# WKV recurrence on one core: another order of the drain, and two pieces of VectorE's work in other places

## The chip, the cores and the metric

The kernel runs on one core of a Trainium2 chip. The metric is the device time of one execution in microseconds (us). The core has a matrix engine (TensorE, "PE" in the profile, with its weight loads as "PEld"), a vector engine (VectorE, "DVE"), an activation engine (ScalarE, "ACT"), a general engine (GpSimd, "POOL") and SyncE ("SP"), which here only issues transfers. Each engine runs its own instructions in program order; semaphores hold an instruction until what it reads or overwrites is ready. Matrix products are written to PSUM, eight banks of 128 partitions by 512 float32. All else on the chip lies in SBUF.

## What is computed

For each of 16 sequences, 2048 steps and 256 channels, the RWKV "WKV" recurrence: a running weighted sum of the values and of the weights, decayed by `w` at each step, with a bonus `u` for the current step.

```python
for t in range(seq_len):
    kk, vv = k[b, t], v[b, t]
    qq = np.maximum(pp, u + kk)
    e1, e2 = np.exp(pp - qq), np.exp(u + kk - qq)
    output[b, t] = (e1 * aa + e2 * vv) / (e1 * bb + e2 + 1e-08)
    qq = np.maximum(pp - w + kk, kk)
    e1, e2 = np.exp(pp - w + kk - qq), np.exp(kk - qq)
    aa, bb, pp = e1 * aa + e2 * vv, e1 * bb + e2, qq
```

`k`, `v` and the output are float32 of 33.6 MB each, so 67.1 MB are read and 33.6 MB written.

## The kernel before

**Tiles.** The 2048 steps are cut into 16 groups of 128 steps (`NST = 16`, index `c`), and the 16 sequences into 4 quadruples, so there are 64 tiles ("pairs" in the code, `NP = 64`, index `n = 4c + p`). A tile is 128 steps by 4 sequences by 256 channels, 512 KB of `k`, of `v` and of output. Inside a tile the recurrence along the 128 steps is done by matrix products with triangular matrices on TensorE; what goes from one group to the next, the carry, is worked out by a chain of small instructions and put into rows of the big buffer `EZR` by four small transfers (`inject`).

**Stages of a tile.** `round_k` (DVE, L176) makes the matmul form of `k`. `logs` (PE, L185 and L191) sums exponents into four PSUM banks, `exps` (ACT, L204) takes their exponential into a slot of the ring `EZR`, `cast_v` (DVE, L209) makes `v` bf16, and `times_v` (DVE, L214) multiplies it in. Ten tiles later (`LAG = 10`), when the carry is in, `den` (PE, L341) makes the denominators in two banks (`DENB`, banks 4 and 5), `recip` (ACT) inverts them as a logarithm (L347) and the exponential of its negative (L349), `num` (PE, L354) makes one half of the numerators in bank 6 (`NUMB`), `mult` (DVE, L358) multiplies that half, and `store` (SP, L361) sends the tile out.

**Carry of group `c`.** `sums` (PE, L238) adds up the group's four tiles in bank 7, `copy_sums` (L246 or L248) copies them, `turn` (PE, L255) transposes, then `state_logs` (ACT, L260), `state_frames`, `state_scan` and `state_offsets` (DVE or POOL, L269 to L286), `state_weights` (ACT, L290), `state_chain` (DVE, L299 to L304), `turn_back` (PE, L320) and `inject` (L326, then four transfers at L331 issued by GpSimd). Each of these is placed by hand at a named slot of a later iteration (the dictionary `later`, L371 to L392; `small_work` runs what is due).

**Order.** Three loops follow one another, and every engine's order is the order of the program. The first (L410, `n` = 0 to 9) has no output work. The second (L431, `n` = 10 to 63) is the steady one: iteration `n` works on tile `n` and on the outputs of `q = n - 10` (denominators and inverse) and `qp = n - 11` (numerators). There, in iterations with `n % 4 == 3` VectorE casts two tiles of `v` (`cast_v(n)` and `cast_v(n + 1)`, L450 to L454), with `n % 4 == 2` none, else one. The third (L477, the drain) only makes the outputs of the tiles that are left, 53 to 63, together with the last group's carry (`c = 15`). In it each iteration runs two tile halves of `num` into banks 0 and 1 or 2 and 3, `recip(q)`, and `den(q + 1)`, which writes the same two banks that `recip(q)` reads.

**Buffers.** SyncE issues in each steady iteration the load of `v` for tile `n + 5`, of `k` for `n + 6` and the store of tile `n - 13`. There are six buffers for `k`, five for `v`, so the load of `v` for `n + 5` waits until `cast_v(n)` has read its buffer, and what follows on SyncE waits behind it. There are eight buffers `rd` for inverses and outputs.

Of the kernel before, what the change touches and what calls it, by code (L numbers as in the profile page):

```python
# [7 lines left out]
F32 = mybir.dt.float32  # L8
# [3 lines left out]
ACT = mybir.ActivationFunctionType  # L12
# [3 lines left out]
def kernel(  # L16
# [9 lines left out]
    K = tc.keep_in_program_order  # L26
# [121 lines left out]
    def out_matrices(*names):  # L148
        if "L" in names:
            for h in range(2):  # L150
                fill(Lx[HS * h:HS * h + HS, HS * (1 - h):HS * (2 - h)], 0.0)
        for name in names:
            x, f = I1 if name[0] == "I" else Lx, RS if name[-1] == "N" else 1.0
            mats[name] = matrix(name, BF16)
            K(DVE.tensor_single_scalar(mats[name], x, f, op=ALU.mult))
# [15 lines left out]
    def ez(n):  # L171
        return EZR[:, :, n % RING]
# [33 lines left out]
    def cast_v(n):  # L206
        vb = vbpool.tile([128, 4, Dm], BF16, tag="vb", name="vb")
        vr = vr_of.pop(n)
        K(DVE.tensor_copy(vb, vr))  # L209
        VB[n] = vb  # L210
# [20 lines left out]
    def sums(n):  # L231
        c, p = divmod(n, 4)
        t = MISC[:, 0:Dm]
        for o in range(2):
            x = 24 - 16 * o - 2 * p
            for j in range(4):
                q, i = divmod(j, 2)
                K(PE.matmul(t[32 * j:32 * j + 32, :], mats["OH"][:, x:x + 32],  # L238
                            ez(n)[:, 2 * q, i, Dm * o:Dm * o + Dm],
                            start=p == 0 and o == 0, stop=p == 3 and o == 1,  # L240
                            tile_position=(0, 32 * j), skip_group_check=True))
# [79 lines left out]
                        skip_group_check=True))  # L321
        st[c, "CT"] = t

    def inject(c):
        cb = small.tile([128, 128], BF16, tag="cb", name="cb")
        K(DVE.tensor_copy(cb, st.pop((c, "CT"))))  # L326
        r0 = 4 * c % RING
        for q in range(2):
            for h in range(2):
                r, x = HS * h + HS - 1, 32 * (2 * q + h)  # L330
                K(POOL.dma_start(  # L331
                    out=EZR[r:r + 1, 2 * q, r0:r0 + 4, :, :].rearrange("o p i (b x) -> o (p i b) x", b=4),
                    in_=cb[x:x + 32, :]))


    RD = {}

    def den(n):
        for m, q in (("L", 0), ("Id", 1)):
            for i in range(2):  # L340
                K(PE.matmul(DENB[:, i, :], mats[m], ez(n)[:, q, i, :], start=q == 0, stop=q == 1,  # L341
                            skip_group_check=True))

    def recip(n, between=lambda: None):
        rd = rpool.tile([128, 2, D], F32, tag="rd", name="rd")
        for i in (slice(0, 1), slice(1, 2)) if n == NP - 1 else (slice(0, 2),):
            K(SC.activation(rd[:, i, :], DENB[:, i, :], ACT.Ln, scale=RS))  # L347
            between()
            K(SC.activation(rd[:, i, :], rd[:, i, :], ACT.Exp, scale=-1.0))  # L349
        RD[n] = rd  # L350

    def num(n, bank, i):
        for m, q in (("LN", 2), ("IdN", 3)):
            K(PE.matmul(bank, mats[m], ez(n)[:, q, i, :], start=q == 2, stop=q == 3, skip_group_check=True))  # L354

    def mult(n, bank, i):
        rd = RD[n]
        K(DVE.tensor_mul(rd[:, i, :], bank, rd[:, i, :]))  # L358

    def store(n):  # L360
        K(SP.dma_start(out=rows_of(out, n), in_=RD.pop(n).rearrange("p i (n d) -> p (i n) d", n=2)))  # L361

    def last_outputs(n, H):
        c, p = divmod(n, 4)
        for i in range(2):
            mult(n, H[:, i, :], i)
            for j, eng in ((0, SP), (1, SC)):
                b = 4 * p + 2 * i + j
                K(eng.dma_start(out=out[b, c * TC:(c + 1) * TC, :], in_=RD[n][:, i, Dm * j:Dm * j + Dm]))

    later = {}  # L371
    for c in range(NST):
        s = 4 * c + 3
        plan = [(s + 1, "act" if s + 1 < LAG else "recip", copy_sums), (s + 1, "pe", turn),
                (s + 2, "act", state_logs), (s + 2, "mid", state_frames), (s + 2, "scan", state_scan), (s + 2, "scan", state_offsets),
                (s + 3, "recip", state_weights), (s + 3, "chain", state_chain),
                (s + 4, "nums", turn_back), (s + 4, "mid", inject), (s + 4, "mid", state_next)]
        if c == 0:
            plan = [(s + 1, "act", copy_sums), (s + 1, "pe", turn), (s + 1, "pe", state_logs),
                    (s + 1, "round", state_frames), (s + 1, "round", state_scan), (s + 1, "round", state_offsets),  # L380
                    (s + 2, "act", state_weights), (s + 2, "round", state_chain),
                    (s + 3, "pe", turn_back), (s + 3, "round", inject), (s + 3, "round", state_next)]
        if c == 1:
            plan = [(s + 1, "act", copy_sums), (s + 1, "pe", turn), (s + 2, "act", state_logs),
                    (s + 2, "round", state_frames), (s + 2, "round", state_scan), (s + 2, "round", state_offsets)] + plan[6:]
        if c == NST - 1:
            plan = [(s + 1, "copy", copy_sums), (s + 1, "turn", turn),
                    (s + 1, "post", state_logs), (s + 1, "mid", state_frames), (s + 1, "mid", state_scan), (s + 1, "mid", state_offsets),
                    (s + 2, "post", state_weights), (s + 2, "first", state_chain),
                    (s + 3, "turn", turn_back), (s + 3, "first", inject)]  # L390
        for slot, where, f in plan:
            later.setdefault((slot, where), []).append((f, c))  # L392

    def small_work(n, where):
        for f, c in later.pop((n, where), []):
            f(c)
# [13 lines left out]
    for n in range(LAG):  # L410

        load(n + AHEAD)
        exps(n)
        if n % 4 == 0 and n:
            sums(n - 1)
        small_work(n, "act")
        small_work(n, "logs")
        logs(n + 1)
        if n % 4:
            sums(n - 1)  # L420
        small_work(n, "pe")
        idle_matmuls(2, NUMB)
        times_v(n)
        small_work(n, "chain")
        round_k(n + 2)
        small_work(n, "round")
        cast_v(n + 1)
        if n < 4:
            (state_start, lambda: out_matrices("L"), lambda: out_matrices("IdN", "LN"),
             lambda: out_matrices("Id"))[n]()  # L430
    for n in range(LAG, NP):  # L431

        q, qp = n - LAG, n - LAG - 1
        load(n + AHEAD)

        if qp >= 2:
            store(qp - 2)
        if qp >= 0:
            num(qp, NUMB, 0)
        den(q)  # L440
        small_work(n, "nums")
        exps(n)
        small_work(n, "act")
        if qp >= 0:
            mult(qp, NUMB, 0)
        small_work(n, "mid")
        if n + 2 < NP:
            round_k(n + 2)

        if n % 4 == 3:  # L450
            cast_v(n)
        if n + 1 < NP:
            if n % 4 != 2:
                cast_v(n + 1)  # L454
        else:
            times_v(n)
        if qp >= 0:
            num(qp, NUMB, 1)

        sums(n - 1)  # L460
        recip(q, lambda: small_work(n, "recip"))
        if qp >= 0:
            mult(qp, NUMB, 1)
        small_work(n, "scan")
        if n + 1 < NP:
            times_v(n)
            small_work(n, "chain")
            logs(n + 1)
        else:
            den(q + 1)  # L470
        small_work(n, "pe")
    sums(NP - 1)
    small_work(NP, "copy")
    late = []
    store(NP - LAG - 3)
    store(NP - LAG - 2)
    for n in range(NP, NP + LAG + 1):  # L477

        q, qp = n - LAG, n - LAG - 1
        H = PS[:, 2 * (n % 2):2 * (n % 2) + 2, :]  # L480
        for i in range(2):
            num(qp, H[:, i, :], i)
        small_work(n, "turn")
        if q < NP:
            recip(q, lambda: small_work(n, "recip"))
        small_work(n, "post")
        if q + 1 < NP:
            den(q + 1)
        small_work(n, "first")
        if qp == NP - 1:  # L490
            last_outputs(qp, H)
            break
        late.append((qp, H))
        if n != NP + 1:

            for x, bank in late:
                mult(x, bank, slice(0, 2))
                store(x)
            late = []
        small_work(n, "mid")  # L500
    assert not later


# [28 lines left out]
```

## Time and profile before

| what | value |
|---|---|
| time, median of three runs | 293.12 us (293.10 to 293.28) |
| span of the profiled execution | 292.3 us |
| DVE busy | 261.9 us, 90% |
| ACT busy | 258.4 us, 88% |
| PE busy | 257.5 us, 88% |
| POOL busy | 113.9 us, 39% |
| `exps` (L204), steady | 54 instructions, 1873 ns each |
| logarithm of a tile (L347) | 1023 ns for 128x1024 |
| exponential of its negative (L349) | 1056 ns for 128x1024 |
| `mult` of one half tile (L358) | 690 ns for 128x512 |
| `cast_v` (L209) | 693 ns |
| bytes moved | 101.53 MB, mean 347 GB/s |

Busy times of an engine are sums over the whole span; the share tells nothing of which stage is limited by what. The timeline has the start and length of each instruction; where the engine was idle just before it, a bracket tells how long and what ended the wait. Two instructions of ACT or DVE can overlap by about 0.1 us in it, so the distance between starts is the better measure of a step. The first loop lasts until about 39 us, the steady one to about 264 us, the drain to the end.

### The profile page before, as it was taken

Reading aid. Unit: us, or ns where it says so; the run is one execution under the profiler, and the core shown is the slowest. Engines: PE = TensorE matmul, PEld = TensorE weight load, DVE = VectorE, ACT = ScalarE, POOL = GpSimd, SP = SyncE. Lnnn points to the kernel's source line nnn. Section 1 sums busy time; section 2 is a strip of 40 time slices with the busy share of each in tenths; the row PEclk is TensorE's granted clock in tenths of the full one; section 3 lists DMA queues with packets and bytes.
Section 4 is the critical chain, followed back from the end, with each engine's and each line's share of the span. In section 5 each row is a group of like instructions: output and inputs, shape, how many; then the busy total and the mean of one; then the engine's idle time right before and its main releaser. Section 6 shows DMA issues by size and latency. Waiting matters only on the chain. (4 is left out here: it accounts for less than half of the span.)

```text
span 292.3 us, 4981 instructions
## 1 busy us (share of the span) xinstructions
PE 257.5 (88%) x1662; PEld 119.7 (41%) x1694; DVE 261.9 (90%) x453; ACT 258.4 (88%) x253; POOL 113.9 (39%) x212
## 2 busy tenths in 40 slices
PE   6976896998989899998989899998989899998881
PEld 2332442534444354444444354444444354433330
DVE  4698989899999999999999999999999999986853
ACT  2765685999999999999999999999999999999892
POOL 7000434153555535253555535253555535242200
PEclk9999997999999999999999999999999999999998
DMA  5999999999999999999999999999999999974686
GB/s 191 356 348 349 348 332 349 334 365 364 378 375 374 380 375 382 379 378 380 380 377 382 380 380 380 377 371 378 379 378 380 370 375 381 370 247 151 222 284 215
DMA packets 103521, 101.53 MB, mean 347 GB/s; under 512 B 4156, under 2 KB 103496, under 8 KB 103496
## 3 DMA queue, kind: packets, MB, share of 16 engines
q1 hardware_dynamic: 101144, 100.42, 100.7%
q0 software_dynamic: 2048, 0.53, 0.8%
q8 instruction: 13, 0.21, 0.3%
q10 hardware_dynamic: 304, 0.27, 0.3%
q14 instruction: 12, 0.10, 0.1%
HBM read 67.12 MB, written 33.55 MB: 344 GB/s over the span
## 5 line engine op out<-in xcount | busy, mean ns | idle before, releaser
L204 ACT ACTIVATE EZR<-PS 128x2048 bf16<-128x2048 f32 x54 | 101.1, 1873 | 7.6 <-PE PS L191 4.9
L358 DVE TENSOR_TENSOR rd<-PS,rd 128x512 f32<-128x512 f32 (+1 forms) x118 | 86.5, 735 | 13.8 <-PE PS L354 7.9
L214 DVE TENSOR_TENSOR EZR<-EZR,vb 128x2048 bf16<-128x2048 bf16 x64 | 78.5, 1227 | 0.7
L349 ACT ACTIVATE rd<-rd 128x1024 f32<-128x1024 f32 (+1 forms) x65 | 67.8, 1043 | 1.2
L347 ACT ACTIVATE rd<-PS 128x1024 f32<-128x1024 f32 (+1 forms) x65 | 65.6, 1010 | 1.4 <-PE PS L341 1.3
L331 POOL DMA_DIRECT2D EZR<-cb x64 | 40.1, 632 | 61.1 <-DVE cb L326 42.3
L354 PE MATMUL PS<-EZR,LN 128*128 128x512 bf16 x128 | 48.7, 380 | 12.8 <-DVE rd L358 10.0
L191 PE MATMUL PS<-km,NLE 128*128 128x512 f32 x128 | 47.2, 450 | 4.1 <-DVE km L176 4.1
L176 DVE CAST km<-kr 128x1024 fp32r<-128x1024 f32 x64 | 44.0, 688 | 2.3 <-DMA kr<-in_k_dram 2.3
L209 DVE CAST vb<-vr 128x1024 bf16<-128x1024 f32 x64 | 43.3, 693 | 2.7 <-DMA vr<-in_v_dram 2.4
L354 PE MATMUL PS<-EZR,IdN 128*128 128x512 bf16 x114 | 43.1, 378 | 0.0
L191 PE MATMUL PS<-km,NLZ 128*128 128x512 f32 x128 | 40.5, 398 | 0.0
L341 PE MATMUL PS<-EZR,L 128*128 128x512 bf16 x127 | 37.8, 378 | 1.8 <-ACT rd L347 1.8
L341 PE MATMUL PS<-EZR,Id 128*128 128x512 bf16 x114 | 35.0, 379 | 0.1
L269 POOL TENSOR_TENSOR F<-LL,LL 128x32 f32<-128x32 f32 x13 | 9.5, 733 | 62.0 <-ACT LL L260 62.0
L185 PE MATMUL PS<-WU,CO 32*128 32x512 bf16 x256 | 27.3, 388 | 3.1 <-DVE WU L406 1.6
L238 PE MATMUL PS<-EZR,OH 128*32 128x256 bf16 x512 | 26.3, 280 | 2.4 <-issue 0.4
L191 PEld LDWEIGHTS PS<-km,NLE 128*128 128x128 f32 x128 | 19.2, 190 | 19.2 <-issue 12.7
L191 PEld LDWEIGHTS PS<-km,NLZ 128*128 128x128 f32 x128 | 24.3, 190 | 5.7
L202 ACT ACTIVATE EZR<-PS 128x1024 bf16<-128x1024 f32 x20 | 19.4, 1019 | 7.9 <-PE PS L191 7.9
L354 PEld LDWEIGHTS <-IdN 128*128 128x128 bf16 x128 | 12.4, 97 | 26.1 <-issue 23.7
L354 PEld LDWEIGHTS <-LN 128*128 128x128 bf16 x128 | 12.8, 100 | 18.5 <-issue 11.5
(71 smaller groups left out, 204.5 us busy)
## 6 DMA issues: line engine op xcount, KB each, us to landing
kr<-in_k_dram SPq DMA_DIRECT2D x64, 512.0 KB, 8.3
vr<-in_v_dram SPq DMA_DIRECT2D x64, 512.0 KB, 8.2
out_dram<-rd SPq DMA_DIRECT2D x63, 512.0 KB, 8.1
EZR<-cb POOLq DMA_DIRECT2D x64, 8.0 KB, 5.2
out_dram<-rd SPq DMA_DIRECT2D x2, 128.0 KB, 3.1
out_dram<-rd ACTq DMA_DIRECT2D x2, 128.0 KB, 3.3
wuf<-in_w_dram ACTq DMA_DIRECT2D x1, 8.0 KB
wuf<-in_u_dram SPq DMA_DIRECT2D x1, 4.0 KB
```

Of the source, the lines that this page charges most:

```text
L176: K(DVE.tensor_copy(km, kr_of.pop(n)))
L185: K(PE.matmul(half(n, q)[:, i, :], CO[g:g + 32, :], WU[g:g + 32, :].unsqueeze(1).broadcast_to([32, 2, Dm]), start=True, stop=False, tile_p ...
L191: K(PE.matmul(half(n, q)[:, i, :], (NLE, NLZ)[q], km[:, i, :], start=False, stop=True, skip_group_check=True))
L204: K(SC.activation(ez(n)[:, 0:2], PS[:, 0:4, :].rearrange("p (q i) x -> p q i x", q=2), ACT.Exp))
L209: K(DVE.tensor_copy(vb, vr))
L214: K(DVE.tensor_mul(ez(n)[:, 2:4], ez(n)[:, 0:2], vb.unsqueeze(1).broadcast_to([128, 2, 2, D])))
L331: K(POOL.dma_start(out=EZR[r:r + 1, 2 * q, r0:r0 + 4, :, :].rearrange("o p i (b x) -> o (p i b) x", b=4), in_=cb[x:x + 32, :]))
L341: K(PE.matmul(DENB[:, i, :], mats[m], ez(n)[:, q, i, :], start=q == 0, stop=q == 1, skip_group_check=True))
L347: K(SC.activation(rd[:, i, :], DENB[:, i, :], ACT.Ln, scale=RS))
L349: K(SC.activation(rd[:, i, :], rd[:, i, :], ACT.Exp, scale=-1.0))
L354: K(PE.matmul(bank, mats[m], ez(n)[:, q, i, :], start=q == 2, stop=q == 3, skip_group_check=True))
L358: K(DVE.tensor_mul(rd[:, i, :], bank, rd[:, i, :]))
```

## The change

There are three edits.

1. **The drain is written out anew.** Denominators alternate between two pairs of banks (4 and 5, then 2 and 3, which hold no exponents any more), numerators go round three banks (0, 1, 6), and ScalarE takes the logarithm of tile `n + 1` before the exponential of tile `n`. It starts at the end of iteration 63: `den(54)` no longer waits for the logarithm of tile 53. The last group's carry is threaded in by hand in another order, and its four small transfers are issued by SyncE instead of GpSimd. The last tile has one logarithm for both halves instead of one for each.
2. **Carry of group 1 and the first inverse.** In iteration 10, the first steady one, `sums` and `recip` come ahead of `round_k(12)`, and `state_chain(1)` follows them at once ("early"), ahead of `round_k` and `times_v` in VectorE's order; before it stood behind both.
3. **One cast moves by an iteration.** `cast_v` of a tile whose number divides by four is done in its own iteration and no longer in the one before: two casts in iterations with `n % 4 == 0`, one with 3, one with 1, none with 2.

```diff
-    def inject(c):
+    def inject(c, queue=POOL):
...
-                K(POOL.dma_start(
+                K(queue.dma_start(
...
         if c == 1:
             plan = [(s + 1, "act", copy_sums), (s + 1, "pe", turn), (s + 2, "act", state_logs),
-                    (s + 2, "round", state_frames), (s + 2, "round", state_scan), (s + 2, "round", state_offsets)] + plan[6:]
+                    (s + 2, "round", state_frames), (s + 2, "round", state_scan), (s + 2, "round", state_offsets),
+                    (s + 3, "recip", state_weights), (s + 3, "early", state_chain)] + plan[8:]
...
+        if n == LAG:
+
+            inverses(n)
+            small_work(n, "early")
         if n + 2 < NP:
             round_k(n + 2)
 
-        if n % 4 == 3:
+        if n % 4 in (3, 0):
             cast_v(n)
-        if n + 1 < NP:
-            if n % 4 != 2:
-                cast_v(n + 1)
-        else:
+        if n + 1 == NP:
             times_v(n)
-        if qp >= 0:
-            num(qp, NUMB, 1)
-
-        sums(n - 1)
-        recip(q, lambda: small_work(n, "recip"))
+        elif n % 4 < 2:
+            cast_v(n + 1)
+        if n > LAG:
+            inverses(n)
...
+    q, c = NP - LAG - 1, NST - 1
+    dbank = lambda n: PS[:, 2:4, :] if (n - q) % 2 else DENB
+    nbank = lambda n, i: PS[:, (0, 1, 6)[(2 * (n - q) + i) % 3], :]
...
+    den_log(q)
+    den(q + 1, dbank(q + 1))
     sums(NP - 1)
...
+    copy_sums(c)
+    store(q - 2)
+    store(q - 1)
+    den_exp(q)
+    den_log(q + 1, dbank(q + 1))
+    tile_num(q, 0)
+    turn(c)
+    state_logs(c)
+    den_exp(q + 1)
+    den(q + 2, dbank(q + 2))
+    den_log(q + 2, dbank(q + 2))
+    tile_num(q, 1)
+    mult(q, nbank(q, 0), 0)
+    state_frames(c)
+    state_scan(c)
+    state_offsets(c)
+    state_weights(c)
+    mult(q, nbank(q, 1), 1)
+    store(q)
+    state_chain(c)
+    den(q + 3, dbank(q + 3))
+    for i in range(2):
+        tile_num(q + 1, i)
+    turn_back(c)
+    inject(c, SP)
+    outputs(q + 1)
+    for n in range(q + 2, NP):
+        if n + 1 < NP:
+            den_log(n + 1, dbank(n + 1))
+        if n + 2 < NP:
+            den(n + 2, dbank(n + 2))
         for i in range(2):
+            tile_num(n, i)
+        if n + 1 < NP:
+            den_exp(n)
+            outputs(n)
+    n, p = NP - 1, (NP - 1) % 4
+    for i in range(2):
+        den_exp(n, slice(i, i + 1))
+        mult(n, nbank(n, i), i)
+        for j, eng in ((0, SP), (1, SC)):
+            b = 4 * p + 2 * i + j
+            K(eng.dma_start(out=out[b, c * TC:(c + 1) * TC, :], in_=RD[n][:, i, Dm * j:Dm * j + Dm]))
```

The function `inverses(n)` holds `num` of the second half, `sums` and `recip`, as they stood in the loop; in iteration 63 it leaves `recip` out, whose parts come in the drain.

More of the change, by code (lines that the diff above doesn't have):

```diff
@@ L336, with den, den_log, den_exp @@
     RD = {}
-    def den(n):
+    def den(n, bank=DENB):
         for m, q in (("L", 0), ("Id", 1)):
             for i in range(2):
-                K(PE.matmul(DENB[:, i, :], mats[m], ez(n)[:, q, i, :], start=q == 0, stop=q == 1,
+                K(PE.matmul(bank[:, i, :], mats[m], ez(n)[:, q, i, :], start=q == 0, stop=q == 1,
                             skip_group_check=True))
[L344 to L350, printed above, removed]
+    def den_log(n, bank=DENB):
+        RD[n] = rpool.tile([128, 2, D], F32, tag="rd", name="rd")
+        K(SC.activation(RD[n], bank, ACT.Ln, scale=RS))
+    def den_exp(n, i=slice(0, 2)):
+        K(SC.activation(RD[n][:, i, :], RD[n][:, i, :], ACT.Exp, scale=-1.0))
+    def recip(n, between):
+        den_log(n)
+        between()
+        den_exp(n)
     def num(n, bank, i):
@@ L361, in store @@
         K(SP.dma_start(out=rows_of(out, n), in_=RD.pop(n).rearrange("p i (n d) -> p (i n) d", n=2)))
[L363 to L369, printed above, removed]
     later = {}
@@ L384 @@
             plan = [(s + 1, "act", copy_sums), (s + 1, "pe", turn), (s + 2, "act", state_logs),
-                    (s + 2, "round", state_frames), (s + 2, "round", state_scan), (s + 2, "round", state_offsets)] + plan[6:]
+                    (s + 2, "round", state_frames), (s + 2, "round", state_scan), (s + 2, "round", state_offsets),
+                    (s + 3, "recip", state_weights), (s + 3, "early", state_chain)] + plan[8:]
         if c == NST - 1:
[L387 to L390, printed above, removed]
+            plan = []
         for slot, where, f in plan:
@@ L430, with inverses @@
              lambda: out_matrices("Id"))[n]()
+    def inverses(n):
+        q, qp = n - LAG, n - LAG - 1
+        if qp >= 0:
+            num(qp, NUMB, 1)
+        sums(n - 1)
+        if n + 1 < NP:
+            recip(q, lambda: small_work(n, "recip"))
     for n in range(LAG, NP):
@@ L468 @@
             logs(n + 1)
-        else:
-            den(q + 1)
         small_work(n, "pe")
-    sums(NP - 1)
[L473 to L480, printed above, removed]
-        for i in range(2):
[L482 to L500, printed above, removed]
+    q, c = NP - LAG - 1, NST - 1
@@ new lines, with outputs @@
+    dbank = lambda n: PS[:, 2:4, :] if (n - q) % 2 else DENB
+    nbank = lambda n, i: PS[:, (0, 1, 6)[(2 * (n - q) + i) % 3], :]
+    tile_num = lambda n, i: num(n, nbank(n, i), i)
+    def outputs(n):
+        for i in range(2):
+            mult(n, nbank(n, i), i)
+        store(n)
+    den_log(q)
+    den(q + 1, dbank(q + 1))
+    sums(NP - 1)
+    copy_sums(c)
[6 more added lines that the diff above has]
+    state_logs(c)
@@ new lines @@
+    den_exp(q + 1)
[21 more added lines that the diff above has]
+            den(n + 2, dbank(n + 2))
+        for i in range(2):
+            tile_num(n, i)
+        if n + 1 < NP:
+            den_exp(n)
+            outputs(n)
@@ L501 @@
+    n, p = NP - 1, (NP - 1) % 4
+    for i in range(2):
+        den_exp(n, slice(i, i + 1))
+        mult(n, nbank(n, i), i)
+        for j, eng in ((0, SP), (1, SC)):
+            b = 4 * p + 2 * i + j
+            K(eng.dma_start(out=out[b, c * TC:(c + 1) * TC, :], in_=RD[n][:, i, Dm * j:Dm * j + Dm]))
     assert not later
```

## The prediction

> **What bounds the kernel now.** I read the page's slices first, then the loads of `k`, then ScalarE's timeline in three places, since the busy shares (88 to 90% for three engines) name no bound.
>
> Clock, DMA share and rate in 40 slices of 7.3 us, from the page:
>
> ```profile
> PEclk9999997999999999999999999999999999999998
> DMA  5999999999999999999999999999999999974686
> GB/s 191 356 348 349 348 332 349 334 365 364 378 375 374 380 375 382 379 378 380 380 377 382 380 380 380 377 371 378 379 378 380 370 375 381 370 247 151 222 284 215
> ```
>
> The DMA engines are busy without a break until slice 35 (256 us), at about 348 GB/s while only loads run and 379 with stores among them. Now the tile `kr` between 200 and 255 us:
>
> ```profile
> L60 SPq DMA_DIRECT2D kr<-in_k_dram x11: 1242/1287/1408, 200.0 to 242.6; - x11
> L176 DVE CAST km<-kr x14: 682/683/684, 200.1 to 253.4; 128x1024 fp32r<-128x1024 f32 x14
> DMA to landing us min/median/max: 8.1/8.3/8.5
> ```
>
> Each issue holds SyncE 1.29 us (0.37 in the drain, by SyncE's own timeline), so the queue pushes back. The last `k` (tile 63) is issued at 242.6 and lands 8.1 to 8.5 later, at 250.7 to 251.1; VectorE takes it at 253.4. Data are early by 2.3 to 2.7 us: the transfers are no wait now, but they stand 2.6 us behind the computation, and SyncE's order is fixed. **This is the ceiling for all that happens before tile 63.**
>
> ScalarE at the start of the steady loop:
>
> ```profile
> 43.60 1.87 ACT L204 ACTIVATE EZR<-PS 128x2048 bf16<-128x2048 f32 x1
> 45.35 1.03 ACT L347 ACTIVATE rd<-PS 128x1024 f32<-128x1024 f32 x1
> 46.42 1.06 ACT L349 ACTIVATE rd<-rd 128x1024 f32<-128x1024 f32 x1
> 50.99 1.88 ACT L204 ACTIVATE EZR<-PS 128x2048 bf16<-128x2048 f32 x1 [3.52 <-PE PS L191]
> ```
>
> A hole of 3.52 us. In a steady cycle of four tiles (16.42 us, again and again), ScalarE, then VectorE:
>
> ```profile
> 164.17 1.06 ACT L349 ACTIVATE rd<-rd 128x1024 f32<-128x1024 f32 x1
> 165.36 1.88 ACT L204 ACTIVATE EZR<-PS 128x2048 bf16<-128x2048 f32 x1
> 167.13 1.02 ACT L347 ACTIVATE rd<-PS 128x1024 f32<-128x1024 f32 x1
> 168.32 0.38 ACT L248 ACTIVATE ts<-PS 128x256 f32<-128x256 f32 x1 [0.17 <-PE PS L238]
> 168.60 1.05 ACT L349 ACTIVATE rd<-rd 128x1024 f32<-128x1024 f32 x1
> 169.76 1.88 ACT L204 ACTIVATE EZR<-PS 128x2048 bf16<-128x2048 f32 x1
> ...
> 176.84 1.04 ACT L349 ACTIVATE rd<-rd 128x1024 f32<-128x1024 f32 x1
> 177.79 1.86 ACT L204 ACTIVATE EZR<-PS 128x2048 bf16<-128x2048 f32 x1
> ```
>
> ```profile
> 163.67 1.29 DVE L209 CAST vb<-vr 128x1024 bf16<-128x1024 f32 x2
> ...
> 165.47 1.22 DVE L214 TENSOR_TENSOR EZR<-EZR,vb 128x2048 bf16<-128x2048 bf16 x1
> ```
>
> Where nothing is missing, an exponential is followed after 0.95 us (176.84 to 177.79); at 164.17 and 168.60 it takes 1.19 and 1.16, and the copy at 168.32 waits for `sums`. In the drain the chain of waits is TensorE L341 and ScalarE L347 in turn, 1.04 and 1.03 us plus 0.06 of issue, 2.13 a tile:
>
> ```profile
> 275.93 1.02 ACT L347 ACTIVATE rd<-PS 128x1024 f32<-128x1024 f32 x1
> 276.99 1.06 ACT L349 ACTIVATE rd<-rd 128x1024 f32<-128x1024 f32 x1
> 278.07 1.02 ACT L347 ACTIVATE rd<-PS 128x1024 f32<-128x1024 f32 x1
> ```
>
> **What the Trainium skill says.** "ScalarE: Activation LUTs", section "What ACT_TABLE_LOAD costs": back-to-back ACTIVATEs overlap by about 93 ns. The trace agrees where the two don't depend on each other (1.06 long, next after 0.95), and shows no overlap where they do or wait. "TensorE: Matmul & The Clock Gate", section "What's actually happening": an idle window of about 3.4 us halves the clock. Here slice 6 and matmuls of L191 at 48.96 us (1.22 us for two, 0.73 elsewhere) show the halving, after an idle stretch of only 2.08 us. "DMA: Bandwidth & Descriptors", section "SWDGE vs HWDGE vs iDMA": the hardware path of SyncE sets up faster than GpSimd's. The trace has no small carry on SyncE; GpSimd's last four take 2.00 us to issue (271.24 to 273.24).
>
> **Part 1, iteration 10.** Now `state_chain(1)` stands behind `round_k(12)` (waits for its data until 43.63) and `times_v(10)`; it ends at 46.53, TensorE has waited 2.08 us for it, and the logs of tile 12 end at 50.95, at half clock. After: the weights end at 42.77, the chain takes 1.15 (45.38 to 46.53), so 43.95; `round_k` starts 0.25 later, `times_v(10)` ends 45.70, `mult(0)` frees the bank at 46.3, `num` 0.6, `sums` 0.4 and logs 1.3 at full clock end at 48.6. Gain 2.4 on ScalarE, 1.2 if the clock is halved all the same (the idle stretch is still 1.4). VectorE, one cast (0.60) lighter in iteration 11, starts tile 12's `mult` 2.0 earlier. I take 2.0.
>
> **Part 2, the cast.** At 163.67 two casts stand ahead of a `mult` and `times_v`. With one, everything behind them is 0.60 earlier: the next `mult` at 166.01 instead of 166.61, so `num`, `sums` and logs of tile 41 by as much. ScalarE then has its copy at 168.05 and the next exponents at 169.28 instead of 169.76. The cast taken up again in iteration 40 lies behind that `mult`, and VectorE idles 0.44 at 170.66, so it is mostly hidden there. Gain 0.46 a cycle, 5.9 over the 12.75 cycles from tile 12 to 63. Price: the load of `v` for tile `n + 5` must now wait for a later cast, and the loads of `k` and the stores stand behind it on SyncE. But the queue holds 8 us of work, and the late cast moves by about 3.5 us at most against a buffer that is free 2 to 7 us before its load is issued. I cost it at nothing.
>
> **Sum before the drain.** 2.0 + 5.9 = 7.9 wanted, but tile 63 can't be rounded before 250.7 to 251.1: **2.6 us is all that can be had** (bounds 2.0 and 3.0, since ScalarE can be slightly further ahead than VectorE). Some 5 us of the gain turn into waits for `k`.
>
> **Part 3, the drain** (in the old times). ScalarE: logarithm 53 at 261.55, exponential at 262.62, logarithm 54 at 263.57 (its denominators are done by 263.3, since they no longer wait). Then `state_logs` comes ahead of exponential 54 and waits: the copy of the sums ends at 264.46, `turn` 0.6 later, so 265.1, a loss of 0.5. Exponential 54 265.25, logarithm 55 266.20, weights 267.10, logarithm 56 267.37, exponential 55 268.46. Logarithm 57 needs `den(57)`, which on TensorE is queued behind `turn_back`, and that behind the chain (weights end 267.45, chain 1.15): `turn_back` ends at 269.0, `den(57)` at 270.0, logarithm at 270.05, a loss of 0.64. From there a logarithm and an exponential of different tiles take 0.95 + 0.90 = 1.85 instead of 2.13: exponential 62 starts at 282.05, the last halves end at 284.15, before 286.75. TensorE needs 8 matmuls by 0.216 = 1.73 a tile and VectorE 1.2, both less. VectorE then has four `mult` of 0.60 from 283.15, ends at 285.63 instead of 287.8. **Gain 2.2**; 1.0 if the overlap doesn't come (2.0 a tile). The carry: cast at 269.3, four issues of at most 0.5 on SyncE, with only `store(54)` behind them; landing takes 1.2 to 2.7 in this stage, so by 274, and `den(60)` is due at 274.3. Stores every 1.85 us are 283 GB/s, under the rate already seen (342).
>
> **Sum.** 293.1 - 2.6 - 2.2 = 288.3.
>
> **Rivals.**
> - *The drain alone gains* (14%): the cast or the early chain gives back what it brings, as VectorE's double iteration now delays `times_v` of the tile divisible by four. For it: VectorE is 96% busy in a cycle (15.83 of 16.42). Against: its idle 0.44. 293.1 - 2.2 = 290.9.
> - *Only the part before the drain gains* (14%): the two waits in part 3 grow, the carry lands behind `store(53)`, or TensorE with banks tied to three `mult` holds `den` back. 293.1 - 2.6 = 290.5.
> - *More* (12%): no wait for `state_logs`, since VectorE is ahead and `times_v(63)` earlier by its 0.6, and ScalarE ahead of VectorE by 3: 293.1 - 3.0 - 2.2 - 0.9 = 287.0.
> - *Slower* (8%): SyncE stands so long at the held `v` load that the queue runs dry. 13 such loads by 0.1 us idle beyond what the queue holds are 1.3, and the drain's waits eat its gain: 294.4.
> - The forecast has 52%.
>
> **The numbers.** The range goes from 286.7 (below "more") to 291.2 (above both one-sided rivals); outside are the slower case and a few per cent of the others. Faster 0.90, within 0.2% 0.03, slower 0.07.
>
> **What would show it.** ScalarE's hole of 3.52 us shrinks to about 1.2; cycles of four between 60 and 150 us take about 16.0 instead of 16.42; later they stretch to the transfers' pace (`k` of tiles 41 and 61 is issued at 149.0 and 233.9, 17.0 a cycle) with waits of VectorE for `kr`, none of which exist now after 80 us; tile 63 is rounded at about 250.8; the drain's logarithms are 1.85 apart; ScalarE waits once for L255 and once for L341. I am wrong if the last `k` lands at another time, if the queue shows slices under 9 before 250 us, or if the drain keeps a step of 2.1.

## The result

| | before | after |
|---|---|---|
| time, median of four runs each | 293.11 us (292.47 to 293.28) | 289.89 us (289.42 to 290.43) |
| span of the profiled execution | 292.3 us | 288.0 us |
| predicted | | 288.3 us (286.7 to 291.2) |

The ratio is 0.9895 (95% interval 0.9871 to 0.9919), so the change saves 3.2 us, where 4.8 were forecast. The profiled execution of before itself took 294.04 us, 0.9 over the median, so part of the 4.3 us by which the two profiles differ comes from that.

**The queue.** From the page of after, in slices of 7.2 us:

```profile
DMA  6999999999999999999999999999999999994697
GB/s 214 353 348 350 349 331 349 331 361 375 381 369 381 372 379 378 381 379 381 378 376 381 369 381 375 377 376 371 373 374 380 374 377 380 373 383 160 201 339 245
```

It is full through slice 36 (35 before), at 348 GB/s for loads alone and about 379 mixed. New is the drain: two thin slices (160 and 201), then 339.

**The last `k`**, tile `kr` from 200 us to 262 us, after; the indented line is how long VectorE sat idle for its data, and how often:

```profile
L176 DVE CAST km<-kr x13: 683/699/795, 199.4 to 250.4; 128x1024 fp32r<-128x1024 f32 x13
L60 SPq DMA_DIRECT2D kr<-in_k_dram x11: 1188/1287/1774, 199.6 to 242.1; - x11
  DMA kr<-in_k_dram: 2.9, 9
DMA to landing us min/median/max: 8.2/8.3/8.5
```

The last load is issued at 242.1 and lands from 250.3 to 250.6; VectorE takes it at 250.4. Before it could wait until 253.4. There is nothing left between landing and use, and in this stretch VectorE now waits for `kr` nine times.

**The start of the steady loop and one cycle**, ScalarE's timeline of after (start, length, instruction; idle time before it in brackets):

```profile
45.59 1.06 ACT L349 ACTIVATE rd<-rd 128x1024 f32<-128x1024 f32 x1
47.86 1.88 ACT L204 ACTIVATE EZR<-PS 128x2048 bf16<-128x2048 f32 x1 [1.21 <-PE PS L191]
...
95.47 1.88 ACT L204 ACTIVATE EZR<-PS 128x2048 bf16<-128x2048 f32 x1
...
111.36 1.88 ACT L204 ACTIVATE EZR<-PS 128x2048 bf16<-128x2048 f32 x1
```

The hole of 3.52 us is 1.21 now (`e6_early_only` below tells how much of that is the change's), and a cycle of four tiles takes 15.89 instead of 16.42. Later cycles stretch to the pace of the transfers: the exponents at the same place of a cycle start at 159.04 and at 175.83, 16.79 apart.

**The drain**, ScalarE's timeline of after (L346 is the logarithm, L349 the exponential, L533 a transfer that ScalarE issues):

```profile
262.31 0.35 ACT L260 ACTIVATE LL<-PS 128x128 f32<-128x128 f32 x1 [0.74 <-PE PS L255]
...
267.31 1.02 ACT L346 ACTIVATE rd<-PS 128x1024 f32<-128x1024 f32 x1 [0.76 <-PE PS L341]
...
274.73 1.04 ACT L346 ACTIVATE rd<-PS 128x1024 f32<-128x1024 f32 x1
275.63 1.08 ACT L349 ACTIVATE rd<-rd 128x1024 f32<-128x1024 f32 x1
276.58 1.05 ACT L346 ACTIVATE rd<-PS 128x1024 f32<-128x1024 f32 x1
...
282.38 0.36 ACTq L533 DMA_DIRECT2D out_dram<-rd  x1
282.80 0.63 ACT L349 ACTIVATE rd<-rd 128x512 f32<-128x512 f32 x1 [1.84 <-DVE rd L362]
```

One wait for `turn` (0.74), one for `den(57)` (0.76), then 1.85 a tile instead of 2.13. New and not foreseen is the end: the second half's exponential could start at 280.8, but ahead of it in ScalarE's order stands the issue of a transfer that waits for the first half's `mult`, and so it starts at 282.80.

### The profile page after: what moved, and what is told of

Same layout as the page of the kernel before. It is cut to its first block, busy times and chain, and to the rows that moved or that the text cites. A ratio compares the mean times of both kernels' runs of the same rounds, so it can differ in the third digit from the quotient of the medians.

```text
span 288.0 us, 5023 instructions
## 1 busy us (share of the span) xinstructions
PE 261.4 (91%) x1694; PEld 119.4 (41%) x1694; DVE 262.3 (91%) x463; ACT 254.7 (88%) x252; POOL 105.2 (37%) x208
## 5 line engine op out<-in xcount | busy, mean ns | idle before, releaser
L362 DVE TENSOR_TENSOR rd<-PS,rd 128x512 f32<-128x512 f32 x128 | 87.0, 687 | 6.1 <-ACT rd L349 4.7
L349 ACT ACTIVATE rd<-rd 128x1024 f32<-128x1024 f32 (+1 forms) x65 | 67.9, 1047 | 2.7 <-DVE rd L362 1.8
L346 ACT ACTIVATE rd<-PS 128x1024 f32<-128x1024 f32 x64 | 65.7, 1026 | 0.8 <-PE PS L341 0.8
L331 POOL DMA_DIRECT2D EZR<-cb x60 | 36.5, 614 | 52.1 <-DVE cb L326 45.4
L176 DVE CAST km<-kr 128x1024 fp32r<-128x1024 f32 x64 | 44.7, 699 | 6.9 <-DMA kr<-in_k_dram 6.4
L191 PE MATMUL PS<-km,NLE 128*128 128x512 f32 x128 | 47.5, 453 | 2.3 <-DVE km L176 2.2
L358 PE MATMUL PS<-EZR,IdN 128*128 128x512 bf16 x128 | 48.4, 378 | 0.0
L191 PE MATMUL PS<-km,NLZ 128*128 128x512 f32 x128 | 40.6, 398 | 0.0
L341 PE MATMUL PS<-EZR,Id 128*128 128x512 bf16 x128 | 38.1, 379 | 0.0
L269 POOL TENSOR_TENSOR F<-LL,LL 128x32 f32<-128x32 f32 x13 | 6.7, 515 | 61.9 <-ACT LL L260 61.9
L191 PEld LDWEIGHTS PS<-km,NLZ 128*128 128x128 f32 x128 | 24.4, 191 | 5.8
L191 PEld LDWEIGHTS PS<-km,NLE 128*128 128x128 f32 x128 | 19.3, 190 | 17.3 <-issue 12.9
L282 POOL TENSOR_TENSOR Q<-P,F 128x64 f32<-128x64 f32 x13 | 15.7, 1205 | 15.0 <-DVE P L273 15.0
```

The costliest lines, as they stand in the source:

```text
L176: K(DVE.tensor_copy(km, kr_of.pop(n)))
L191: K(PE.matmul(half(n, q)[:, i, :], (NLE, NLZ)[q], km[:, i, :], start=False, stop=True, skip_group_check=True))
L331: K(queue.dma_start(out=EZR[r:r + 1, 2 * q, r0:r0 + 4, :, :].rearrange("o p i (b x) -> o (p i b) x", b=4), in_=cb[x:x + 32, :]))
L341: K(PE.matmul(bank[:, i, :], mats[m], ez(n)[:, q, i, :], start=q == 0, stop=q == 1, skip_group_check=True))
L346: K(SC.activation(RD[n], bank, ACT.Ln, scale=RS))
L349: K(SC.activation(RD[n][:, i, :], RD[n][:, i, :], ACT.Exp, scale=-1.0))
```

## The experiments

Each kernel was timed beside the kernel before, on the same chip; ratios are to that, with the 95% interval. "After" stands for 0.9895. Two theories were to be told apart from others. **The cap**: what comes before the drain can gain only until the last `k` is taken as it lands. **ScalarE at the end**: the drain lost part of its gain to the wait of 1.84 us.

### The parts alone

`e1_drain_only` has the new drain, and the loops as they were:

```diff
...
-        if n == LAG:
-
-            inverses(n)
-            small_work(n, "early")
...
-        if n % 4 in (3, 0):
+        if n % 4 == 3:
             cast_v(n)
...
-        elif n % 4 < 2:
+        elif n % 4 != 2:
             cast_v(n + 1)
...
```

> The new drain alone; early chain and cast as before. Theory A (the part before the drain is capped by the landing of the last k, some 2 us below the time before; in the drain the new order wins 2.2 us, and 1.2 of it are lost again because a transfer issued by ScalarE stands between the last two exponentials): 293.1 - 1.0 = 292.1. Rival B (the drain is the whole gain, the two small moves bring nothing): 289.9. Rival C (the drain's own waits eat its gain, the small moves bring all): 293.1.

Measured 291.60 us, ratio 0.9951 (0.9931 to 0.9970), which is 1.4 us and lies between A and B. Its loops are those of before, so its profile shows once more when they take the last `k`:

```profile
L176 DVE CAST km<-kr x14: 682/683/687, 199.4 to 252.8; 128x1024 fp32r<-128x1024 f32 x14
```

That is 2.4 us later than after (250.4), not 3.0 as the first profile of before had it.

`e2_old_drain` is the other half, early chain and moved cast with the drain as before.

> Early chain and moved cast with the drain as before. A: the cap on what comes before the drain is 2.0 us, so 291.1, and VectorE waits for kr in the last third. B: 293.1. C: 289.9.

Measured 291.36 us, ratio 0.9938 (0.9920 to 0.9955), 1.8 us. VectorE takes the last `k` at 250.2 us and waits for `kr` seven times from 200 us on, as A had it. The two halves together, 1.4 + 1.8, are the 3.2 of the whole.

`e5_cast_only` moves the cast alone:

```diff
-        if n % 4 == 3:
+        if n % 4 in (3, 0):
             cast_v(n)
         if n + 1 < NP:
-            if n % 4 != 2:
+            if n % 4 < 2:
                 cast_v(n + 1)
```

> Only the cast moved. A (cap): the cast alone would bring 0.5 us in each of 12 cycles, so it reaches the cap by itself: 293.1 - 2.0 = 291.1, as with both small moves. Rival (no cap, parts add up): its share of 2 us, about 1.5, and the early chain the other 0.5: 291.6.

Measured 291.52 us, ratio 0.9943 (0.9921 to 0.9965), 1.7 us, almost all that both moves bring. Both times that were named, 291.1 and 291.6, lie in its interval. VectorE takes the last `k` at 250.7 us.

`e6_early_only` has the early chain alone:

```diff
...
+        if n == LAG:
+            sums(n - 1)
+            recip(q, lambda: small_work(n, "recip"))
+            small_work(n, "early")
         if n + 2 < NP:
             round_k(n + 2)
...
-        sums(n - 1)
-        recip(q, lambda: small_work(n, "recip"))
+        if n > LAG:
+            sums(n - 1)
+            recip(q, lambda: small_work(n, "recip"))
```

> Only the early chain of group 1. A (cap): ScalarE's hole of 3.5 us shrinks to about 1.2, a lead of some 2.2 us is kept to the end and just reaches the cap: 293.1 - 2.0 = 291.1, no less than the cast alone. Rival (parts add up to the 2 us that both bring): 0.5, so 292.6.

Measured 292.58 us, ratio 0.9988 (0.9968 to 1.0007): 0.4 us, not told from nothing, and not the 2.0 that I expected. In its profile the last `k` is taken at 251.6, 1.2 before `e1_drain_only` (252.8), and VectorE doesn't wait for `kr`. So between these two profiles the lead is about 1.2, short of the cap.

Not even that is all the early chain's, since the hole at the start of the steady loop depends on the execution. With the loops of before it is 3.52 us in the profile of before and 2.71 in that of `e1_drain_only`, but 1.66 in `e8_before_two_more` and 1.48 in `e12_before_two_copies`, two kernels described below, which at this point still run as before does. From `e12_before_two_copies`, TensorE and then ScalarE:

```profile
45.65 0.40 PE L320 MATMUL PS<-Id,CB 128*128 128x128 bf16 x4 [2.50 <-DVE CB L304]
47.34 0.74 PE L191 MATMUL PS<-km,NLE 128*128 128x512 f32 x2
48.57 1.88 ACT L204 ACTIVATE EZR<-PS 128x2048 bf16<-128x2048 f32 x1 [1.48 <-PE PS L191]
```

In the first two TensorE's clock was halved just then (two matmuls of L191 take 1.22 us), in the last two it was not (0.72 and 0.74). Against 1.48 and 1.66 the 1.20 of `e6_early_only`, at whole clock too, is a gain of 0.3 to 0.5, about what the times say.

These four runs alone don't decide between a cap and parts that add up (0.4 + 1.7 against 1.8, each uncertain by half a microsecond or more).

### The cap

`e7_after_two_more` and `e8_before_two_more` were to put 1 MB more into the queue by sending tiles 12 and 16 out twice:

```diff
...
+        for _ in range(2 if n in (12, 16) else 1):
+            K(SP.dma_start(out=rows_of(out, n), in_=rd))
```

> The changed kernel with two stores more: the outputs of tiles 12 and 16 are sent out twice, same data to the same place, which puts 1 MB or 2.8 us more into the queue ahead of the last loads. A (cap by the last k): the whole of it comes through, 289.9 + 2.7 = 292.6. Rival (the queue has room, the engines bound): 290.1 at most.

> The kernel before with the same two stores more. A: it has about 2 us between the last k and its use, so only 0.8 of the 2.8 come through: 293.9. Rival (transfers bound it already): 295.9. Rival (engines bound both): 293.2.

Measured 302.14 us, 1.0312 (1.0291 to 1.0333), and 303.20 us, 1.0352 (1.0330 to 1.0375). Both missed by far, for a reason of their own: writing the same place twice makes SyncE wait until the first transfer has landed. From the waits of SyncE in the first of them (us in total, times, longest):

```profile
SPq L367 <- DMA out_dram<-rd: 13.8, 2, 7.1
```

`e8_before_two_more` has the same wait, 13.8 us in two. With SyncE held for 7 us each time, the loads behind it come late in both. They say nothing of the cap. In their place I took copies from memory to memory that nothing waits for:

```diff
+        if n in (30, 34):
+            K(SP.dma_start(out=rows_of(out, NP - 3 + (n == 34)), in_=rows_of(k, n)))
```

> The changed kernel with two copies of 512 KB each more in SyncE's queue (k tiles 30 and 34, from memory to memory, to places of the output that are written over at the end), in iterations 30 and 34. Unlike the doubled stores they wait for nothing. Cap by the last k: 2.8 us more in the queue come through almost whole, 289.9 + 2.5 = 292.4. Rival (engines bound): within 0.4 of 289.9.

> The kernel before with the same two copies. With 2 to 3 us between landing and use of the last k: at most 0.8 us more, 293.1 to 293.9. Rival (transfers already bind the kernel before): 295.7.

Measured 292.44 us, ratio 0.9984 (0.9973 to 0.9994), for after with the copies, which is 2.6 us more than after; and 293.47 us, ratio 1.0017 (1.0005 to 1.0030), for before with them, 0.5 us more. Tile `kr` from 200 us, first after with the copies, then before with them:

```profile
L176 DVE CAST km<-kr x13: 683/695/750, 202.0 to 253.0; 128x1024 fp32r<-128x1024 f32 x13
```

```profile
L176 DVE CAST km<-kr x13: 682/694/795, 202.4 to 253.3; 128x1024 fp32r<-128x1024 f32 x13
  DMA kr<-in_k_dram: 1.2, 5
```

The last `k` is taken at 253.0 in the one (250.4 without the copies), at 253.3 in the other (252.8 in `e1_drain_only`), where VectorE begins to wait for it. The same load on the queue costs the changed kernel about five times what it costs the kernel before, which had room for most of it. This shows the cap.

The other way round, `e9_stores_later` takes stores out of the way of the loads, each store two iterations later from the start (with the order of `e3_tail` below at the end):

```diff
-    kpool = ctx.enter_context(tc.tile_pool(name="kpool", bufs=AHEAD))
+    kpool = ctx.enter_context(tc.tile_pool(name="kpool", bufs=5))
...
-    vbpool = ctx.enter_context(tc.tile_pool(name="vbpool", bufs=4))
-    rpool = ctx.enter_context(tc.tile_pool(name="rpool", bufs=8))
+    vbpool = ctx.enter_context(tc.tile_pool(name="vbpool", bufs=3))
+    rpool = ctx.enter_context(tc.tile_pool(name="rpool", bufs=10))
...
-        if qp >= 2:
-            store(qp - 2)
+        if qp >= 4:
+            store(qp - 4)
...
```

> The changed kernel with the last exponentials as in e3 and each store two iterations later (ten output buffers instead of eight, paid for with one k buffer and one bf16 v buffer less), so that two stores fewer stand ahead of the last k. A (cap): last k lands 2.8 us earlier, and the computation, which had 5 us of lead to give, follows: 288.7 - 2.7 = 286.0. Rival (engines bound; the cap is not the queue): 288.7. Rival (fewer k buffers delay loads): over 289.

Measured 290.06 us, ratio 0.9894 (0.9861 to 0.9927): nothing gained. Most of the reason is in the tenth slice of its page, 65 to 72 us, and SyncE's waits between 60 and 75 us name it:

```profile
GB/s 219 352 348 350 349 331 350 332 343 268 369 367 376 379 379 382 375 372 366 376 373 381 377 380 375 379 373 365 377 378 379 369 382 375 376 383 279 179 338 239
```

```profile
SPq L64 <- DVE vb L209: 5.4, 2, 4.5
```

With no stores to issue, SyncE comes to the loads of `v` before VectorE has freed their buffers, stands for up to 4.5 us, and the queue loses (375 - 268) GB/s over 7 us, 0.75 MB, the worth of almost 1.5 of the two stores. Its last `k` is issued at 242.4 us, no earlier than after (242.1), so the cap was not moved. So `e10_two_stores_held` holds two stores back where the queue is deep, in iterations 36 and 37, with the same buffers and the end as in after:

```diff
-        if qp >= 2:
-            store(qp - 2)
+        late = 2 if n >= 38 else 0
+        if qp >= 2 and n not in (36, 37):
+            store(qp - 2 - late)
...
-    store(q - 2)
-    store(q - 1)
+    for x in range(q - 4, q):
+        store(x)
```

> The changed kernel with two stores held back in the middle: none in iterations 36 and 37, and from 38 on each store two iterations later, so that two stores fewer stand ahead of the last k; ten output buffers, one k buffer and one bf16 v buffer less. Stores of e9, later from the start, left a gap in the queue at 64 to 72 us; here the queue is full by then. Cap by the last k: it lands 2.7 us earlier, at about 247.7, and the time falls from 289.9 to about 287.5. Rival (engines bound, or the held stores come back whole at the end, where stores follow one another at 340 GB/s): 289.9.

Measured 287.86 us, ratio 0.9825 (0.9809 to 0.9842): 5.1 us under the kernel before and 2.1 under after. Tile `kr` from 200 us:

```profile
L176 DVE CAST km<-kr x12: 677/683/791, 201.9 to 247.4; 128x1024 fp32r<-128x1024 f32 x12
```

The last `k` is taken at 247.4, 3.0 earlier than after, and 2.1 of it reach the end; the drain, where the held stores come back, is 0.7 longer (31.9 us from the last exponents of the loop to the end of the span, 31.2 in after). No engine does less work in it, and the buffers are those of `e9_stores_later`, which gained nothing: what bound was the place of the loads in the queue. This version beats both.

### The end of the drain

`e3_tail` takes both exponentials of the last tile ahead of the transfers that ScalarE issues:

```diff
     for i in range(2):
         den_exp(n, slice(i, i + 1))
+    for i in range(2):
         mult(n, nbank(n, i), i)
```

> The changed kernel with both exponentials of the last tile ahead of its first mult and of the transfers that ScalarE issues. A: the wait of 1.84 us ahead of the last exponential goes, the last mult starts 1.2 us earlier, so 289.9 - 1.2 = 288.7. Rival (the stores still in the queue set the end, with 340 GB/s from 272 us on): within 0.3 of 289.9.

Measured 290.50 us, ratio 0.9919 (0.9891 to 0.9946): no gain over 0.9895. ScalarE's end in it:

```profile
279.58 2.14 ACT L349 ACTIVATE rd<-rd 128x1024 f32<-128x1024 f32 x3
282.63 1.33 ACTq L534 DMA_DIRECT2D out_dram<-rd  x2
```

The wait of 1.84 us is gone, the last exponential ends at 281.72 instead of 283.42 and the last `mult` at 283.20 instead of 284.15, and yet the span ends at 288.3 instead of 288.0. My theory of the drain's end fell. That the stores set the end is not yet shown by this run alone, since SyncE issues the store of tile 62 no earlier in it (282.07 us, 281.82 in after).

`e13_log_behind` keeps the two pairs of banks, and takes the logarithm of a tile behind the exponential of the one before:

```diff
     for n in range(q + 2, NP):
-        if n + 1 < NP:
-            den_log(n + 1, dbank(n + 1))
...
             den_exp(n)
+            den_log(n + 1, dbank(n + 1))
             outputs(n)
```

> The changed kernel with the two pairs of denominator banks kept, but in the drain's loop the logarithm of tile n + 1 behind the exponential of tile n. Within a tile the exponential then follows its own logarithm after 1.05 us, and the next logarithm after 0.95: 2.0 a tile instead of 1.85, over eight tiles 1.2 us on ScalarE; if ScalarE sets the end, 291.1. Rival (the stores set the end, which follow at 340 GB/s): under 290.4.

Measured 289.71 us, ratio 0.9894 (0.9878 to 0.9910), the same as after, with a step of 2.0 on ScalarE:

```profile
275.24 1.00 ACT L346 ACTIVATE rd<-PS 128x1024 f32<-128x1024 f32 x1
276.28 1.06 ACT L349 ACTIVATE rd<-rd 128x1024 f32<-128x1024 f32 x1
277.24 1.01 ACT L346 ACTIVATE rd<-PS 128x1024 f32<-128x1024 f32 x1
```

But the step did not make the outputs late, as I had expected: each exponential now stands ahead of the next logarithm, and the last whole one starts at 278.28 us, where it was 279.34 in after. Counted from the store of tile 54, the store of tile 62 is issued after 11.64 us (12.43 in after) and the last `mult` ends after 14.35 (14.76). None of this reaches the end of the span, 18.54 us after that store (18.56 in after). So the last work of ScalarE and VectorE does not set the end here; what a later ScalarE would cost, no run shows. What sets it is seen in the stretch from 272 to 284 us, busy time by engine, then clock, DMA share and GB/s, first before, then after:

```profile
272.00:284.00 12.00, 10.76 (x47) 4.47 (x46) 7.82 (x7) 11.29 (x12) 1.24 (x3) 1.00 0.86 285
```

```profile
272.00:284.00 12.00, 8.70 (x39) 3.52 (x36) 8.12 (x13) 9.58 (x12) 0.00 (x0) 1.00 1.03 340
```

Before, the stores had room (share 0.86); after, the queue is full again, at 340 GB/s with stores alone. SyncE issues the store of tile 54 at 269.39 us, right behind the four carries. VectorE's four `mult` of tiles 54 and 55, the carries and the first stores, after:

```profile
266.65 2.48 DVE L362 TENSOR_TENSOR rd<-PS,rd 128x512 f32<-128x512 f32 x4
266.77 2.52 SPq L331 DMA_DIRECT2D EZR<-cb  x4
269.39 2.17 SPq L365 DMA_DIRECT2D out_dram<-rd  x3
```

From there to the end 9 tiles of 524 KB and the last one remain, 5.24 MB, 15.4 us at 340 GB/s; what is left of the 18.56, 3.2 us, is start, landing and end. The distance from this store to the end of the span is 18.56 us in after, 18.73 in `e3_tail`, 18.54 in `e13_log_behind`, 18.54 in `e10_two_stores_held`, 18.46 in `e1_drain_only` and 18.34 in `e11_after_two_copies`. So the drain's end is set by when the store of tile 54 starts and by the rate of stores. The products follow close behind, though. Reckoned from the store of tile 62 with the same rate and the same 3.2, the end comes out at 281.82 + 3.1 + 3.2 = 288.1 in after, no other than measured, and at 287.0 in `e13_log_behind`, earlier than the 287.6 measured; in that run the two limits stand apart, and the stores from tile 54 on are the later one.

Why the store of tile 54 starts when it does can be read from the lines above. Its two products are ready at about 267.9, and SyncE is still issuing the carries, until 269.28. In the kernel before, where GpSimd issued them, this store left at 271.85, as soon as its product was ready (about 271.8). Counted from the last exponents of the loop, it leaves after 12.62 us in after and after 12.05 before. So moving the carries to SyncE holds this store back by some 1.4 us. No run put them back on GpSimd. By the sum of 288.1 an earlier start of this store alone would bring little in after.

## Where the prediction was right and where not

- **The reading of the bound held.** The queue is full until the drain, the last `k` lands 0.4 to 0.5 us ahead of the time named from the profile of before (250.7 to 251.1; it was 250.3 to 250.6), it is taken as it lands, and the copies and held stores show that this binds. Cycles fell to 15.89 (16.0 named), and later ones stretched to 16.79 (17.0 named).
- **The size of the cap, 2.6, was too large.** The gap was read from one execution, which took 0.9 us over the median. Its first `v` was cast at 9.55 us (8.52 in after's), and TensorE's clock was halved in it near 47 us: between the exponents of tiles 11 and 12 lie 7.39 us in it, 6.58 in `e1_drain_only` and, at whole clock, 5.33 in `e12_before_two_copies`. So its computation ran late. `e1_drain_only`, with the same loops, takes its last `k` at 252.8, and the trace then gives 2.4. The times say 1.8 (1.3 to 2.3, `e2_old_drain`). An execution at whole clock should leave a smaller gap, but none with these loops and no extra transfers was profiled, so what lies between the two is not settled.
- **Part 1 was too large alone.** I took 2.0 for the early chain; its profile shows 1.2, the lower bound of that step, and the times 0.4. The hole of 3.52 that it was to close was that of an execution at half clock. At whole clock the loops of before have 1.48 or 1.66, and 1.2 remain with the early chain. Nor did the change cure the halving: the clock stayed whole in after's profile, but `e9_stores_later` and `e10_two_stores_held`, with the same early chain, have it halved there, and holes of 1.61 and 2.01. The moved cast brings almost all there is. Since both meet the same cap, the error left no mark on the sum, which is luck.
- **The step that failed is the drain's "Gain 2.2".** On ScalarE its parts came near: waits of 0.74 and 0.76 where 0.5 and 0.64 were named, and a step of 1.85. But it took the end of VectorE's work for the end of the kernel, with the same tail behind it as before. Counted from the start of the last exponents of the loop, the last `mult` ends after 28.0 us before and after 26.2 in `e3_tail`, 1.8 gained; the span ends after 32.5 and 31.3, only 1.2 gained. In after it ends after 31.2: 1.35 gained (1.4 by the times of `e1_drain_only`). The stores were checked only by their mean pace (283 GB/s under 342), and the four carries on SyncE, seen to have the store of tile 54 behind them, were put at nothing for it. They hold it back, the first three stores come in a bunch (269.39, 270.01 and 270.88), the queue is full from 272 us on, and the end comes 18.6 us after the store of tile 54. How much of the missing 0.8 that delay costs stays open, since reckoned from the store of tile 62 the end comes out the same. The unforeseen wait of ScalarE costs nothing for the same reason.
- **The sum:** forecast 2.6 + 2.2 = 4.8; measured 1.8 + 1.4 = 3.2. Both terms were 0.8 too large, with no error of the other sign.
- **The carries by SyncE** take 2.52 us for the four (266.77 to 269.28), more than GpSimd's 2.00 before; the faster set-up that the Trainium skill names for that path ("DMA: Bandwidth & Descriptors", section "SWDGE vs HWDGE vs iDMA") doesn't show in the time that these small transfers take to issue. They land 1.8 to 1.9 us after their issue, the last at about 270.6, which is no wait: `den(60)` starts at 271.43 us.

Of the rivals, "slower" and "more" didn't come. "Drain alone" and "before the drain alone" are each contradicted by the two halves, which gained about alike.

## What to carry to other kernels

Where a full transfer queue runs beside full engines, work out for the last load when it lands and when it is used. Here that gap was all that faster engines could gain, and moving two stores out from ahead of that load brought 2.1 us more, as much as the whole part before the drain had. Do the same for the last stores: bytes left over the rate, from the time that the first of them can start, before a faster producer is credited, and look at what stands ahead of that first one on the engine that issues it. And take a gap of a few microseconds from more than one execution: one hole, in the same loops, was 3.52, 2.71, 1.66 and 1.48 us in four.

## What the runs showed of the hardware

- ScalarE: two activations of different tiles follow one another after 0.90 to 0.95 us at lengths of 1.02 and 1.06 (after), and an exponential follows its own logarithm after 1.04 to 1.05 (`e13_log_behind`).
- The queue moved 348 GB/s with loads alone, about 380 with loads and stores mixed, and 340 with stores alone.
- The length of one idle stretch did not decide over TensorE's clock. Near 47 us it was halved after an idle stretch of 2.08 us (before), 2.06 (`e1_drain_only`), 1.82 (`e10_two_stores_held`) and 1.71 (`e9_stores_later`), and stayed whole after 2.50 (`e12_before_two_copies`), 1.86 (`e8_before_two_more`) and 1.74 (after). One that was halved, from `e10_two_stores_held`, with two matmuls of L191 behind it that take 0.73 us at whole clock:

```profile
46.10 0.38 PE L358 MATMUL PS<-EZR,LN 128*128 128x512 bf16 x1 [1.82 <-DVE rd L362]
...
47.28 1.15 PE L191 MATMUL PS<-km,NLE 128*128 128x512 f32 x2
```

- An issue of a transfer that waits on ScalarE's queue held back the activation behind it, for 1.84 us (after).
